# Gate row summed from two rounded parts, and square sums added by VectorE: a change to a hybrid linear-attention trunk on one Trainium2 core

## The chip, the cores and the metric

The kernel runs on one core of one Trainium2 chip. The metric is the device time of one execution in microseconds (us). Three runs of the kernel before gave 1219.83, 1215.38 and 1220.5 us; their median is 1219.83 us.

A core has five engines that work side by side, each through its own queue in order: TensorE (PE) for matrix products, with its weight loads listed as PEld; VectorE (DVE) and ScalarE (ACT) for elementwise work; GpSimd (POOL), which can also add and here mostly issues stores; SyncE (SP), which issues loads. They meet through semaphores. Where one engine's instruction waits, everything behind it in that engine's queue waits too.

## The reference, cut to what matters

```python
def reference(x, c, ada_w, ada_b, ...):
    c_act = silu(c)
    mod = c_act @ ada_w + ada_b
    shift, scale, gate = split(mod, 3)
    h = rms_norm(x, norm_w) * (1 + scale) + shift
    hq, hf, hi, hz, gq, gk, gv, gz, ga, mg = split(h @ w_in, IN_OFFSETS)
    y_h = hgrn2_branch(hq, hf, hi, hz, ...)   # 8 heads, one RMS norm over all 1024 columns
    y_g = gla_branch(gq, gk, gv, gz, ga, ...) # 4 heads of 256, an RMS norm in each head
    merged = sigmoid(mg[0]) * (y_h @ w_branch[0]) + sigmoid(mg[1]) * (y_g @ w_branch[1])
    x = x + gate * (merged @ w_out)
    return rms_norm(x, final_norm_w)
```

The sequence has 1024 rows of 1024 columns; everything is float32. Two pieces matter here. The row `gate` is the last third of `silu(c) @ ada_w + ada_b`, 1024 numbers. The two RMS norms of the branches need, for each row of the sequence, the sum of the squares of the heads' outputs.

## The kernel before

Large products are made from numbers split in two parts: `split` (lines 191 to 198) lets ScalarE round a tile to the type float32r (`hi`, line 196) and VectorE subtract that from the tile (`lo`, line 197). A product then takes three matmuls (hi·hi, hi·lo, lo·hi), each of them a single instruction in the trace. Tiles that are not split go to TensorE as plain float32.

The program has three stretches. First comes a prologue in a fixed order (up to about 110 us of the span), which makes the modulation and the first projections. Then `Stream.go` (line 884) runs a list of projection jobs on TensorE (lines 541, 600 to 602, 643 to 645). After each unit of a job, `weave` (line 895) lets side work go one step: the attention of the heads (`stream.side`), and behind it `stream.back`, which holds the gate row and the preparation of factors and weight sums. A generator's `yield n` asks for n units before its next step, so it sets where its next instructions come in the program. Last come the branch products (line 1343) and the output stage (line 1520). A scheduler then orders each engine's instructions; buffers are 46 slots of 4 KB per partition, taken in rotation by `Slots`.

Three places are touched.

- `gate_side` (lines 1044 to 1065) makes the gate row. SyncE loads eight tiles of `ada_w` (line 1050) and the bias row (line 1047). VectorE weights each tile by its part of `silu(c)` and sums the eight into `gacc` (lines 1052 and 1054). That leaves a sum over 128 partitions. TensorE does it in two halves of 512 columns by a matmul with a tile of ones (line 1062) and adds the bias by a matmul of one partition (line 1063), both in plain float32. ScalarE copies the result out (line 1064). `gate_b` is used much later, in `gate_wy` (line 1471).
- `gla_attention` (line 970): for each of four heads ScalarE squares the two halves of 128 columns (line 981), VectorE scales the outputs (line 982), and GpSimd adds the two tiles of squares (line 987). `inverse_root` (line 957) then splits the sum (lines 196 and 197), sums it over the partitions by two matmuls for each half with the float32r tile of ones, `ones_r` (lines 964 and 965), and takes the root.
- `hgrn_attention` (line 1086): for each of eight heads ScalarE squares (line 1095), VectorE scales (line 1096), and from the second head on GpSimd adds the squares to a running sum (line 1107). After the eighth, `inverse_root` follows.

Other VectorE work that is named below: lines 676 to 701 prepare a head's scores, line 953 multiplies a projection with its sigmoid, lines 1261, 1264 and 1286 are the second parts of the splits for the branch products, line 1166 makes factors.

Of the kernel before, what the change touches and what calls it, by code (L numbers as in the profile page):

```python
# [83 lines left out]
def hybrid_trunk_kernel(  # L84
# [6 lines left out]
    nc = tc.nc  # L91
# [9 lines left out]
    S = Slots(sp, N_SLOTS)  # L101
# [7 lines left out]
    def mtile():  # L109
        cnt[0] += 1  # L110
        return ps_m.tile([P, 512], F32, tag="m", name=f"pm{cnt[0]}")
# [6 lines left out]
    ones = cp.tile([P, P], F32, name="ones")  # L118
# [6 lines left out]
    ones_r = cp.tile([P, P], F32R, name="ones_r")  # L125
# [65 lines left out]
    def split(src, hi=None, lo=None):  # L191

        if hi is None:
            hi = S.get(list(src.shape[1:]), F32R)
            lo = S.get(list(src.shape[1:]), F32R)
        nc.scalar.copy(hi, src)  # L196
        nc.vector.tensor_sub(lo, src, hi.bitcast(F32))  # L197
        return hi, lo
# [715 lines left out]
    def put_act(acts, d, y):  # L914
        for half in range(2):
            nc.gpsimd.dma_start(acts[half][d // 2][:, d % 2 * 512:d % 2 * 512 + 512], y[:, half * 512:half * 512 + 512])
        S.free(y)
# [39 lines left out]
    def inverse_root(dst, sq, n):  # L957

        hi, lo = split(sq)
        yield 1  # L960
        for half in range(2):
            sl = slice(half * 512, half * 512 + 512)
            pn = mtile()
            nc.tensor.matmul(pn, ones_r, hi[:, sl], start=True, stop=False)
            nc.tensor.matmul(pn, ones_r, lo[:, sl], start=False, stop=True)
            nc.scalar.activation(dst[:, sl], pn, AF.Ln, bias=eps_t, scale=1.0 / n)
        nc.scalar.activation(dst, dst, AF.Exp, scale=-0.5)
        S.free(hi, lo)

    def gla_attention(h):  # L970
        qk = g_state
        v = qk.pop(("v", h))
        g = {}
        sq = {}

        def post(vh, half, po):
            if half == 0:
                g[vh] = qk.pop(("z", h, vh))
                sq[vh] = S.get([T])
            sl = slice(half * 512, half * 512 + 512)  # L980
            nc.scalar.activation(sq[vh][:, sl], po, AF.Square)
            nc.vector.scalar_tensor_tensor(g[vh][:, sl], po, vec[:, R_GN + vh:R_GN + vh + 1],
                                           g[vh][:, sl], ALU.mult, ALU.mult)

        yield from attention(qk.pop(("q", h)), qk.pop(("k", h)), alphas[h], lambda: v, 0, 256, post)
        S.free(*v)
        nc.gpsimd.tensor_add(sq[0], sq[0], sq[1])
        yield 1.5
        rst = sq[1]
        yield from inverse_root(rst, sq[0], 256)  # L990
        for half in range(4):
            sl = slice(half * 256, half * 256 + 256)
            for vh in range(2):
                nc.vector.tensor_mul(g[vh][:, sl], g[vh][:, sl], rst[:, sl])
            yield 1.5
        for vh in range(2):
            put_act(yg_d, 2 * h + vh, g[vh])
        S.free(*sq.values())
# [32 lines left out]
    for h in range(4):  # L1031
        if h >= 2:
            J.append(Feat(col(C_GK + h * P), rhs_h, gla_k_done(h)))
        J.append(Feat(col(C_GZ + h * 256), rhs_h, silu_done(g_state, ("z", h, 0))))
        J.append(Feat(col(C_GZ + h * 256 + P), rhs_h, silu_done(g_state, ("z", h, 1))))

        def v_done(v, h=h):
            g_state[("v", h)] = v
            start_side(gla_attention(h))
        J.append(Vblk(C_GV + h * 256, v_done))  # L1040
# [3 lines left out]
    def gate_side():  # L1044

        gacc, gbias = S.get([D]), S.get([D])
        nc.sync.dma_start(gbias[0:1, :], ada_b[0:1, 2 * D:3 * D])
        for k in range(KT):
            b = S.get([D])
            nc.sync.dma_start(b, ada_w[0, k * P:(k + 1) * P, 2 * D:3 * D])  # L1050
            if k == 0:
                nc.vector.tensor_scalar_mul(gacc, b, cs[:, 0:1])
            else:
                nc.vector.scalar_tensor_tensor(gacc, b, cs[:, k:k + 1], gacc, ALU.mult, ALU.add)
            S.free(b)
            yield 1
        yield 3
        gate_b[0] = S.get([D])
        for half in range(2):
            sl = slice(half * 512, half * 512 + 512)  # L1060
            pg = mtile()
            nc.tensor.matmul(pg, ones, gacc[:, sl], start=True, stop=False)
            nc.tensor.matmul(pg, ones[0:1, :], gbias[0:1, sl], start=False, stop=True)
            nc.scalar.copy(gate_b[0][:, sl], pg)
        S.free(gacc, gbias)


    h_state = {}
    ssq, rst_h = [None], [None]
# [16 lines left out]
    def hgrn_attention(h):  # L1086
        st = h_state
        y = [None]
        sq = [None]

        def post(vh, half, po):
            if half == 0:
                y[0], sq[0] = st.pop(("z", h)), S.get([T])
            sl = slice(half * 512, half * 512 + 512)
            nc.scalar.activation(sq[0][:, sl], po, AF.Square)
            nc.vector.scalar_tensor_tensor(y[0][:, sl], po, vec[:, R_HN + h:R_HN + h + 1],
                                           y[0][:, sl], ALU.mult, ALU.mult)

        yield from attention(st.pop(("q", h)), st.pop(("k", h)), st.pop(("f", h)), lambda: st[("v", h // 4)],
                             h % 4 * P, P, post, 4 if h % 4 == 1 else 3)  # L1100
        if h % 4 == 3:
            S.free(*st.pop(("v", h // 4)))
        put_act(yh_d, h, y[0])
        if ssq[0] is None:
            ssq[0] = sq[0]
        else:
            nc.gpsimd.tensor_add(ssq[0], ssq[0], sq[0])
            S.free(sq[0])
        if h == 7:
            yield 2  # L1110
            rst = S.get([T])
            yield from inverse_root(rst, ssq[0], D)
            S.free(ssq[0])
            rst_h[0] = rst

    def hgrn_v(h):
        def done(v):
            h_state[("v", h // 4)] = v
            if h == 0:
                stream.back.append([gate_side(), 4])  # L1120
        J.append(Vblk2(C_HI + h * P, done, lambda: start_side(hgrn_attention(h), 4)))

    for h in range(8):
        J.append(Feat(col(C_HQ + h * P), rhs_h, hq_done(h)))

        def f_done(ps, h=h):
            hf_done(h)(ps)
            if h % 4:
                start_side(hgrn_attention(h), 2)
        J.append(Feat(col(C_HF + h * P), rhs_h, f_done))  # L1130
        if h % 4 == 0:
            hgrn_v(h)
        J.append(Feat(col(C_HZ + h * P), rhs_h, silu_done(h_state, ("z", h))))
# [585 lines left out]
```

## Time and profile before

The profiled execution took 1216.46 us; its span, from the first instruction to the last, is 1214.8 us, so 1.7 us lie around it.

| | |
|---|---|
| median of three runs | 1219.83 us (1215.38 to 1220.5) |
| profiled execution, time and span | 1216.46 us, 1214.8 us |
| granted TensorE clock, mean | 0.998 |
| busy: TensorE, weight loads | 97 %, 81 % |
| busy: VectorE, ScalarE, GpSimd | 65 %, 45 %, 10 % |
| line 1062 and 1063, plain float32 | 2 matmuls each, 4 records each in the trace |

In the profile, a row of a timeline gives the start, the busy time, the engine, the line, the operation and the tiles, and in brackets how long the engine had been idle and what ended that. Busy times of one engine overlap, since the next instruction starts before the last result is written: what an instruction costs its engine is the step from its start to the next start. A row of waits reads: who waited for whom, the total, how many times, the longest.

### The profile page before, as it was taken

Reading aid. Unit: us, or ns where it says so; the run is one execution under the profiler, and the core shown is the slowest. Engines: PE = TensorE matmul, PEld = TensorE weight load, DVE = VectorE, ACT = ScalarE, POOL = GpSimd, SP = SyncE. Lnnn points to the kernel's source line nnn. Section 1 sums busy time; section 2 is a strip of 40 time slices with the busy share of each in tenths; the row PEclk is TensorE's granted clock in tenths of the full one; section 3 lists DMA queues with packets and bytes.
Section 4 is the critical chain, followed back from the end, with each engine's and each line's share of the span. In section 5 each row is a group of like instructions: output and inputs, shape, how many; then the busy total and the mean of one; then the engine's idle time right before and its main releaser. Section 6 shows DMA issues by size and latency. Waiting matters only on the chain.

```text
span 1214.8 us, 20860 instructions
## 1 busy us (share of the span) xinstructions
PE 1184.1 (97%) x8579; PEld 982.6 (81%) x8579; DVE 790.9 (65%) x1245; ACT 546.9 (45%) x797; POOL 123.8 (10%) x215
## 2 busy tenths in 40 slices
PE   5999999999999999999999999999999999999997
PEld 3777889889798888888887888877778888878886
DVE  4637444774848456877884365794653775988994
ACT  5646732434434244344332324455743544444554
POOL 4100000202111121121110101011220000000000
PEclk9999999999999999999999999999999999999999
DMA  9814000844444267255341112054697746435523
GB/s 320 277 70 139 18 19 19 293 141 161 156 152 149 66 207 249 94 179 169 108 174 47 59 53 70 36 174 158 227 343 277 260 160 208 135 104 173 174 104 122
DMA packets 130961, 183.51 MB, mean 151 GB/s; under 512 B 7467, under 2 KB 97633, under 8 KB 130866
## 3 DMA queue, kind: packets, MB, share of 16 engines
q1 hardware_dynamic: 117250, 136.87, 35.7%
q0 software_dynamic: 13568, 45.31, 9.6%
q8 instruction: 67, 1.10, 0.4%
q14 instruction: 28, 0.23, 0.1%
q10 hardware_dynamic: 48, 0.01, 0.0%
HBM read 132.87 MB, written 49.28 MB: 150 GB/s over the span
## 4 chain that ended last, share of the span: by engine, by line
PE 61%; issue 23%; DVE 3%; ACT 3%; POOL 2%; DMA 1%; POOLq 0%; ACTq 0%; DVEq 0%
PE pd L541 19%; PE pd L1343 9%; PE sc_ps L1343 5%; PE pm L1343 5%; PE pd L1520 3%; PE pd L643 2%; PE pd L644 2%; PE pd L645 2%; PE sc_ps L1520 2%; PE pm L848 1%; PE pd L352 1%; PE pm L829 1%; PE pm L850 1%; PE pm L1520 1%; PE sc_ps L352 1%
## 5 line engine op out<-in xcount | busy, mean ns | idle before, releaser
L541 PE MATMUL pd<-b,b 128*128 128x512 f32 x1632 | 387.4, 394 | 0.0
L541 PEld LDWEIGHTS pd<-b,b 128*128 128x128 f32 x1632 | 302.4, 188 | 64.8 <-issue 1.4
L1343 PE MATMUL pd<-b,b 128*128 128x512 f32 x720 | 173.7, 392 | 4.3 <-ACT b L1414 2.1
L1343 PEld LDWEIGHTS pd<-b,b 128*128 128x128 f32 x720 | 133.7, 188 | 35.7 <-ACT b L1414 3.2
L197 DVE TENSOR_TENSOR b<-b,b 128x1024 fp32r<-128x1024 f32 (+2 forms) x89 | 98.9, 1122 | 83.1 <-ACT b L196 65.4
L196 ACT CAST b<-b 128x1024 fp32r<-128x1024 f32 (+2 forms) x89 | 82.9, 948 | 92.1 <-DVE b L1199 14.6
L1286 DVE TENSOR_TENSOR b<-b,b 128x1024 fp32r<-128x1024 f32 x56 | 68.3, 1224 | 66.9 <-ACT b L1285 52.3
L1285 ACT CAST b<-b 128x1024 fp32r<-128x1024 f32 x56 | 58.3, 1050 | 73.9 <-PE pd L1343 20.6
L1343 PE MATMUL sc_ps<-b,b 128*128 128x512 f32 x324 | 79.4, 391 | 1.0 <-ACT scT L793 1.0
L600 PE MATMUL pd<-b,b 128*128 128x256 f32 x256 | 74.2, 290 | 0.0
L1264 DVE TENSOR_TENSOR b<-b,b 128x1024 fp32r<-128x1024 f32 x48 | 59.2, 1251 | 20.8 <-ACT b L1263 15.1
L602 PE MATMUL pd<-b,b 128*128 128x256 f32 x256 | 72.5, 283 | 0.0
L601 PE MATMUL pd<-b,b 128*128 128x256 f32 x256 | 72.4, 283 | 0.0
L1343 PEld LDWEIGHTS sc_ps<-b,b 128*128 128x128 f32 x324 | 60.3, 188 | 14.6 <-ACT scT L793 1.4
L1343 PE MATMUL pm<-b,b 128*128 128x512 f32 x300 | 72.1, 389 | 0.0
L1263 ACT CAST b<-b 128x1024 fp32r<-128x1024 f32 x48 | 49.9, 1050 | 41.2 <-PE pd L1343 16.0
L1343 PEld LDWEIGHTS pm<-b,b 128*128 128x128 f32 x300 | 56.3, 188 | 11.7
L352 PE MATMUL pd<-b,b 128*128 128x512 f32 x192 | 53.3, 410 | 2.0 <-ACT b L196 0.9
L1201 POOL DMA_DIRECT2D ws<-b x64 | 34.6, 541 | 192.0 <-DVE b L1195 86.5
L735 ACT COPY xb<-b 128x512 f32<-128x512 f32 x48 | 29.4, 620 | 49.4 <-PE sc_ps L715 26.7
L643 PE MATMUL pd<-b,b 128*128 128x512 f32 x128 | 51.3, 401 | 0.0
L644 PE MATMUL pd<-b,b 128*128 128x512 f32 x128 | 50.0, 390 | 0.0
(285 smaller groups left out, 1964.3 us busy)
## 6 DMA issues: line engine op xcount, KB each, us to landing
b<-in_w_in_dram SPq DMA_DIRECT2D x66, 512.0 KB, 4.2
ws<-b POOLq DMA_DIRECT2D x64, 256.0 KB, 3.3
b<-ws SPq DMA_DIRECT2D x32, 512.0 KB, 4.9
b<-in_x_dram SPq DMA_DIRECT2D x16, 512.0 KB, 5.7
b<-in_ada_w_dram SPq DMA_DIRECT2D x32, 256.0 KB, 6.9
b<-in_w_branch_dram SPq DMA_DIRECT2D x16, 512.0 KB, 4.4
b<-h SPq DMA_DIRECT2D x14, 512.0 KB, 4.3
wo<-b POOLq DMA_DIRECT2D x14, 512.0 KB, 5.7
```

The source lines that it names most:

```text
L196: nc.scalar.copy(hi, src)
L197: nc.vector.tensor_sub(lo, src, hi.bitcast(F32))
L352: nc.tensor.matmul(accs[f], wg(a, d, f), b[d][:, half * 512:half * 512 + 512], start=(d == 0 and n == 0), stop=(d == KT - 1 and n == 2))
L541: nc.tensor.matmul(ps[0:w, th * 512:(th + 1) * 512], a[:, k, 0:w], b[:, th * 512:(th + 1) * 512], start=(k == 0 and n == 0), stop=(k == KT ...
L600: nc.tensor.matmul(o, lh, hi[:, k % 4, :], start=(k == 0), stop=False)
L601: nc.tensor.matmul(o, lh, lo[:, k % 4, :], start=False, stop=False)
L602: nc.tensor.matmul(o, ll, hi[:, k % 4, :], start=False, stop=(k == KT - 1))
L643: nc.tensor.matmul(o, lh, hi[:, k % 2, :], start=(k == 0), stop=False)
L644: nc.tensor.matmul(o, lh, lo[:, k % 2, :], start=False, stop=False)
L1286: nc.vector.tensor_sub(lo, t, hi.bitcast(F32))
L1343: nc.tensor.matmul(o, a[:, sl], c, start=(p in (1, 5) and kt == 0 and n == 0), stop=(kt == 3 and n == 2), skip_group_check=True)
L1520: nc.tensor.matmul(o, a, b, start=(p in (1, 5) and kt == 0 and n == 0), stop=(kt == 3 and n == 2), skip_group_check=True)
```

## The change

The bias row is added to partition 0 of `gacc` by VectorE. `gacc` is then split, and each half of the column sums is two matmuls with `ones_r`, one for each part. The pause before them is 4 units where it was 3. The additions of squares at lines 987 and 1107 go from GpSimd to VectorE. Lines behind line 1057 stand three lines later in the changed kernel.

```diff
-        nc.gpsimd.tensor_add(sq[0], sq[0], sq[1])
+        nc.vector.tensor_add(sq[0], sq[0], sq[1])
...
-        yield 3
+        nc.vector.tensor_add(gacc[0:1, :], gacc[0:1, :], gbias[0:1, :])
+        hi, lo = split(gacc)
+        S.free(gacc, gbias)
+        yield 4
         gate_b[0] = S.get([D])
         for half in range(2):
             sl = slice(half * 512, half * 512 + 512)
             pg = mtile()
-            nc.tensor.matmul(pg, ones, gacc[:, sl], start=True, stop=False)
-            nc.tensor.matmul(pg, ones[0:1, :], gbias[0:1, sl], start=False, stop=True)
+            nc.tensor.matmul(pg, ones_r, hi[:, sl], start=True, stop=False)
+            nc.tensor.matmul(pg, ones_r, lo[:, sl], start=False, stop=True)
             nc.scalar.copy(gate_b[0][:, sl], pg)
-        S.free(gacc, gbias)
+        S.free(hi, lo)
...
-            nc.gpsimd.tensor_add(ssq[0], ssq[0], sq[0])
+            nc.vector.tensor_add(ssq[0], ssq[0], sq[0])
```

TensorE's queue at the gate row, before: the tiles `pm` are the two halves of the row, b_5918 is `gacc`, b_5919 the bias, and `pd` are the projections of a value block.

```order
L645 MATMUL pd_5955<-b_5711,b_158 128x512
L1062 MATMUL pm_6017<-b_5918,ones 128x512
L1063 MATMUL pm_6017<-b_5919,ones 128x512
L1062 MATMUL pm_6021<-b_5918,ones 128x512
L1063 MATMUL pm_6021<-b_5919,ones 128x512
L643 MATMUL pd_6026<-b_5699,b_143 128x512
```

The same place in the changed kernel, where b_5999 is `hi` and b_6000 `lo`:

```order
L645 MATMUL pd_5955<-b_5711,b_158 128x512
L643 MATMUL pd_6022<-b_5699,b_143 128x512
L644 MATMUL pd_6022<-b_5700,b_143 128x512
L645 MATMUL pd_6022<-b_5699,b_151 128x512
L643 MATMUL pd_6022<-b_5699,b_144 128x512
L644 MATMUL pd_6022<-b_5700,b_144 128x512
L645 MATMUL pd_6022<-b_5699,b_152 128x512
L1065 MATMUL pm_6030<-b_5999,ones_r 128x512
L1066 MATMUL pm_6030<-b_6000,ones_r 128x512
L1065 MATMUL pm_6034<-b_5999,ones_r 128x512
L1066 MATMUL pm_6034<-b_6000,ones_r 128x512
L643 MATMUL pd_6022<-b_5703,b_145 128x512
```

The four matmuls of the row have moved behind six matmuls of the next value block; the rest of TensorE's queue is in the same order as before.

VectorE's queue ahead of them, before, where the line 1054 rows sum the row into `gacc`:

```order
L1054 SCALAR_TENSOR_TENSOR b_5918<-b_5933,cs,b_5918 128x1024
L1096 SCALAR_TENSOR_TENSOR b_5489<-pm_5891,vec,b_5489 128x512
L686 TENSOR_TENSOR b_5669<-xb,b_5848 128x256x3
L688 TENSOR_TENSOR b_5848<-b_5848 128x256
L701 TENSOR_TENSOR tot_725<-b_5848 128x256
L1054 SCALAR_TENSOR_TENSOR b_5918<-b_5942,cs,b_5918 128x1024
L197 TENSOR_TENSOR b_6331<-b_5855,b_6330 128x1024
L1054 SCALAR_TENSOR_TENSOR b_5918<-b_5951,cs,b_5918 128x1024
```

And in the changed kernel, from the same instruction on to the split of `gacc` (line 1110 is the addition of squares that was at line 1107):

```order
L1054 SCALAR_TENSOR_TENSOR b_5918<-b_5933,cs,b_5918 128x1024
L1099 SCALAR_TENSOR_TENSOR b_5489<-pm_5891,vec,b_5489 128x512
L1110 TENSOR_TENSOR b_4458<-b_4458,b_5888 128x1024
L686 TENSOR_TENSOR b_5669<-xb,b_5848 128x256x3
L688 TENSOR_TENSOR b_5848<-b_5848 128x256
...
L1054 SCALAR_TENSOR_TENSOR b_5918<-b_5971,cs,b_5918 128x1024
L197 TENSOR_TENSOR b_6336<-b_5855,b_6335 128x1024
L1054 SCALAR_TENSOR_TENSOR b_5918<-b_5980,cs,b_5918 128x1024
L1054 SCALAR_TENSOR_TENSOR b_5918<-b_5989,cs,b_5918 128x1024
L1057 TENSOR_TENSOR b_5918<-b_5918,b_5919 1x1024
L197 TENSOR_TENSOR b_6000<-b_5918,b_5999 128x1024
```

Three instructions are new between the first term of the row and TensorE: an addition of squares (line 1110), the addition of the bias (line 1057) and the split's subtraction (line 197 into b_6000), which waits for a rounding on ScalarE. The split into b_6336 has moved behind the fifth of the seven line 1054 rows; before, it stood behind the second.

VectorE's queue at the start of the branch products, before and after the addition of the seventh head's squares; before:

```order
L1096 SCALAR_TENSOR_TENSOR b_7051<-pm_7354,vec,b_7051 128x512
L679 TENSOR_TENSOR xb<-xb,b_7329 128x32x8
L1286 TENSOR_TENSOR b_7443<-b_7181,b_7442 128x1024
L686 TENSOR_TENSOR b_7164<-xb,b_7329 128x256x3
L687 TENSOR_TENSOR b_7329<-b_7329 128x256
```

And in the changed kernel (line 1289 is the former line 1286):

```order
L1099 SCALAR_TENSOR_TENSOR b_7056<-pm_7359,vec,b_7056 128x512
L1110 TENSOR_TENSOR b_4458<-b_4458,b_7356 128x1024
L679 TENSOR_TENSOR xb<-xb,b_7334 128x32x8
L1289 TENSOR_TENSOR b_7448<-b_7186,b_7447 128x1024
L686 TENSOR_TENSOR b_7169<-xb,b_7334 128x256x3
```

The addition stands ahead of twelve instructions that end with line 953, and six of those twelve are splits for the branch products, as before.

## The prediction

> **What bounds the kernel now.** I read the page first: which engine is busy, and what the chain that ended last is made of.
>
> ```profile
> PE 1184.1 (97%) x8579; PEld 982.6 (81%) x8579; DVE 790.9 (65%) x1245; ACT 546.9 (45%) x797; POOL 123.8 (10%) x215
> PE 61%; issue 23%; DVE 3%; ACT 3%; POOL 2%; DMA 1%; POOLq 0%; ACTq 0%; DVEq 0%
> ```
>
> TensorE is busy for 97 % of the span, and 84 % of the last chain is TensorE or its issue. So what an instruction costs on TensorE's queue counts in full; what it costs elsewhere counts where TensorE waits for it. The waits of TensorE come second; these rows are the longest one and the two longest behind the prologue.
>
> ```profile
> PE pm L219 <- DVE b L210: 8.3, 4, 4.0
> ...
> PE pd L1343 <- ACT b L1414: 2.1, 2, 1.8
> PE pd L1343 <- DVE b L953: 1.5, 1, 1.5
> ```
>
> The first belongs to the prologue, which the change does not touch. The last is the only one of over 1 us for VectorE in the rest, and it matters below. Third is the timeline where the change is.
>
> **The gate row on TensorE.** Its queue at the row:
>
> ```profile
> 640.92 1.02 PE L1062 MATMUL pm<-b,ones 128*128 128x512 f32 x2
> 641.87 1.12 PE L1063 MATMUL pm<-b,ones 1*128 1x512 f32 x2
> 642.92 1.12 PE L1062 MATMUL pm<-b,ones 128*128 128x512 f32 x2
> 643.98 1.12 PE L1063 MATMUL pm<-b,ones 1*128 1x512 f32 x2
> 645.02 0.50 PE L643 MATMUL pd<-b,b 128*128 128x512 f32 x1
> 645.36 0.39 PE L644 MATMUL pd<-b,b 128*128 128x512 f32 x1
> ```
>
> Four plain float32 matmuls hold the queue from 640.92 to 645.02, 4.10 us, and the bias of one partition costs as much as the 128 (1.05 us). The next step is 0.34 us. The new form runs already in the eighth head's `inverse_root`:
>
> ```profile
> 854.39 0.40 PE L964 MATMUL pm<-b,ones_r 128*128 128x512 f32 x1
> 854.62 0.47 PE L965 MATMUL pm<-b,ones_r 128*128 128x512 f32 x1
> 854.93 0.40 PE L964 MATMUL pm<-b,ones_r 128*128 128x512 f32 x1
> 855.16 0.39 PE L965 MATMUL pm<-b,ones_r 128*128 128x512 f32 x1
> 855.39 4.28 PE L1343 MATMUL sc_ps<-b,b 128*128 128x512 f32 x18
> ```
>
> One step is 0.23 us, so the new four cost 0.92 us (1.00 with the small hold inside this group). The long step after the old row (0.34 against 0.23) goes as well. The term is 0.92 - 4.10 - 0.11 = **-3.3 us**.
>
> [...]
>
> **Does TensorE wait for the two parts?** The row now needs three more steps on VectorE and ScalarE. VectorE's rows before:
>
> ```profile
> 624.44 1.28 DVE L1054 SCALAR_TENSOR_TENSOR b<-b,cs,b 128x1024 f32<-128x1024 f32 x1
> 625.63 0.75 DVE L1096 SCALAR_TENSOR_TENSOR b<-pm,vec,b 128x512 f32<-128x512 f32 x1
> 626.29 2.51 DVE L686 TENSOR_TENSOR b<-xb,b 128x768 f32<-128x768 f32 x1
> ...
> 631.27 1.23 DVE L197 TENSOR_TENSOR b<-b,b 128x1024 fp32r<-128x1024 f32 x1
> 632.41 6.56 DVE L1054 SCALAR_TENSOR_TENSOR b<-b,cs,b 128x1024 f32<-128x1024 f32 x5
> ```
>
> `gacc` is done at 638.97. GpSimd's addition and the group of line 686 explain the long third row:
>
> ```profile
> 624.37 3.62 POOL L1107 TENSOR_TENSOR b<-b,b 128x1024 f32<-128x1024 f32 x1
> L686 DVE TENSOR_TENSOR b<-xb,b x12: 940/952/2508, 117.1 to 802.3; 128x768 f32<-128x768 f32 x12
> ```
>
> Line 686 takes 0.95 us in the median and 2.51 us here, next to an addition on GpSimd that ends at 627.99. So GpSimd's addition holds up VectorE's instruction, and with it gone line 686 gets back 1.56 us. In its place VectorE does the addition itself: one step of a tile of 1024, 631.27 to 632.41, is 1.14 us. The end of `gacc` moves to 638.97 + 1.14 - 1.56 = 638.55. [...]
>
> The trace has no addition over one partition; its bounds are 0 and the 1.22 us of a whole tile (below). I take 1.22, since TensorE's one-partition row cost as much as its full one. A rounding and its subtraction, and what ScalarE does at that time:
>
> ```profile
> 613.51 1.05 ACT L196 CAST b<-b 128x1024 fp32r<-128x1024 f32 x1
> 614.59 1.23 DVE L197 TENSOR_TENSOR b<-b,b 128x1024 fp32r<-128x1024 f32 x1 [5.55 <-ACT b L196]
> 641.12 1.01 ACT L648 COPY b<-pd 128x1024 f32<-128x1024 f32 x1 [9.86 <-PE pd L645]
> ```
>
> ScalarE was idle for 9.86 us up to 641.12, so it can round at once. Then `hi` is there at 638.55 + 1.22 + 1.05 = 640.8 and `lo` at 642.1. TensorE comes to the first new matmul six steps later than before, at 640.92 + 6 x 0.23 = 642.3, and needs `lo` at 642.5: no wait, with 0.4 us in hand. Ahead of the rounding on ScalarE stands one rounding that needs the third weighted tile, some 6 us earlier; behind it only the copy of line 648, whose bank is needed only a whole block of 48 matmuls later. If line 686 keeps its 2.51 us, `lo` comes at 643.6 and TensorE and all behind it wait 1.1 us: bounds 0 and +1.1, taken 0.
>
> **The eleven additions.** GpSimd before, and a same-sized addition on VectorE:
>
> ```profile
> L987 POOL TENSOR_TENSOR b<-b,b x4: 2390/2403/3028, 216.1 to 422.4; 128x1024 f32<-128x1024 f32 x4
> L1107 POOL TENSOR_TENSOR b<-b,b x7: 2395/2405/3617, 532.6 to 849.6; 128x1024 f32<-128x1024 f32 x7
> L1166 DVE TENSOR_TENSOR b<-b,b x8: 1214/1224/1227, 221.0 to 250.6; 128x1024 f32<-128x1024 f32 x8
> ```
>
> GpSimd loses at least 11 x 2.4 = 26 us of work, VectorE gains 11 x 1.14 = 12.5 us. The chain of squares gets 1.2 us shorter each time, but TensorE hardly waits at its end (no row of `inverse_root` is among its longer waits). In eleven stretches, each over one of GpSimd's additions, TensorE was busy all the time:
>
> ```profile
> sum 34.00, PE 34.00 PEld 29.37 DVE 26.15 ACT 12.90 POOL 30.90; mean PE 3.09 PEld 2.67 DVE 2.38 ACT 1.17 POOL 2.81
> ```
>
> So I count ten at nothing: VectorE has 65 % of the span busy, TensorE's queue covers it. If that cover is gone, each costs up to 1.14 us. No new addition waits long: each stands behind the scaling of the same output, which has waited for the same squares. GpSimd's stores no longer stand behind an addition, and SyncE's queue keeps its order but for one pair of loads near the first attention.
>
> The seventh head's addition is different. It stands ahead of the VectorE work for which TensorE waits:
>
> ```profile
> 798.04 2.75 POOL L1107 TENSOR_TENSOR b<-b,b 128x1024 f32<-128x1024 f32 x1
> 799.10 2.21 DVE L679 TENSOR_TENSOR xb<-xb,b 128x256 f32<-128x256 f32 x1
> 810.62 1.23 DVE L953 TENSOR_TENSOR b<-b,pd 128x1024 f32<-128x1024 f32 x1
> 811.90 3.47 PE L1343 MATMUL pd<-b,b 128*128 128x512 f32 x14 [1.49 <-DVE b L953]
> L679 DVE TENSOR_TENSOR xb<-xb,b x12: 637/656/2352, 115.9 to 799.1; 128x256 f32<-128x256 f32 x12
> 796.00:812.00 16.00, 14.51 (x125) 11.59 (x124) 15.97 (x18) 10.95 (x13) 3.79 (x3) 1.00 0.71 244
> ```
>
> In the last row the fourth number is VectorE: 15.97 of 16 us. Here VectorE is the bound, and TensorE stands for 1.49 us. The change adds 1.14 us there and gives back 2.21 - 0.66 = 1.55 us: **-0.4 us**; bounds +1.14 (nothing given back) and -1.5 (the wait gone).
>
> **Sum**: -3.3 - 0.4 = -3.7 us on the profiled execution: 1216.46 becomes 1212.8 us. The median of the three runs is 3.4 us above that execution, and the runs spread over 5.1 us; I carry the difference to the median: 1219.83 - 3.7 = **1216.1 us**, 0.3 % less.
>
> **The rivals.**
>
> - [...] Several of GpSimd's additions held VectorE; if without them TensorE's remaining waits in the body shrink too (1.49, 2.1 and smaller ones), up to 3 us more go: 1213 us. For: the long rows of 679 and 686. Against: ScalarE ends the 2.1.
> - *TensorE waits for the low part.* 1.1 us, and the 798 us place gives nothing: 1217.6 us. For: only 0.4 us in hand. Against: the row above.
> - *TensorE gains nothing by coming earlier.* The 3.3 us are given back at the next wait for a load, or the new form costs as much as the old: 1219.8 us. Against: lines 964 and 965, and waits that follow TensorE themselves.
> - *Slower: VectorE's queue becomes the bound.* The additions come ahead of what TensorE waits for, as they do at 798 us, and nothing is given back. All eleven would add 12.5 us, less 3.3: 1229 us. It decides from 0.3 us of TensorE wait for each addition, and passes 0.5 % at 0.86 us. For: the row from 796 to 812. Against: ten of the eleven places. [...]
>
> **How the numbers follow.** Forecast 50 %, more from the interface 18 %, the low part 15 %, nothing gained 12 %, slower 5 %. A measurement of this kernel tells about 0.5 % (6.1 us) from no change. Faster by more than that needs the first rival or a low median: 0.20; within 0.75; slower 0.05. The range reaches from the first rival with 2 us of run spread, 1211, to nothing gained with 1.2 us, 1221; the last rival is left out.
>
> **What would show it.** Right: lines 1065 and 1066 with one record each, four steps of about 0.23 us, no wait ahead of line 1066; lines 679 and 686 with no row over 1.2 us; TensorE's wait for line 953 at 1.1 us or less; 26 us or more less of GpSimd, and VectorE's busy time up by less than the 13 steps of 1.14 us (14.8 us) that it takes on, since long rows shrink. Wrong: a gap before line 1066, or new waits of TensorE for VectorE behind any of lines 987 and 1110.

## The result, and the profile after

The changed kernel takes **1212.3 us** (median of 12 runs, 1211.28 to 1215.76); the kernel before, on the same chip beside it, 1216.5 us (12 runs, 1214.52 to 1220.5). The ratio is 0.9967, with a 95 % interval of 0.9956 to 0.9979: 0.33 % or 4 us faster, where 3.7 us (0.30 %) was forecast. That is below the 0.5 % that I had named as the bound, so by my cases it is "within 0.5 %", but the interval leaves out 1.

The profiled execution of the changed kernel took 1213.82 us, with a span of 1212.1 us. Its busy times (engine, us, share of the span, instructions):

```profile
PE 1182.6 (98%) x8575; PEld 983.5 (81%) x8575; DVE 793.2 (65%) x1258; ACT 547.6 (45%) x798; POOL 95.5 (8%) x204
```

GpSimd (POOL) loses 28.3 us. VectorE took on thirteen steps of about 1.14 us, 14.8 us, and is busy only 2.3 us longer: 12.5 us came back from instructions that GpSimd's additions no longer hold up. Where they had been held, the groups of single lines (shortest/median/longest in ns) now show no long row:

```profile
L679 DVE TENSOR_TENSOR xb<-xb,b x12: 639/650/660, 115.8 to 795.8; 128x256 f32<-128x256 f32 x12
L686 DVE TENSOR_TENSOR b<-xb,b x12: 941/948/977, 117.0 to 797.5; 128x768 f32<-128x768 f32 x12
L1110 DVE TENSOR_TENSOR b<-b,b x7: 1203/1216/1225, 532.4 to 847.1; 128x1024 f32<-128x1024 f32 x7
```

The longest rows before were 2352 ns (679) and 2508 ns (686). The row on TensorE, from its timeline:

```profile
641.20 0.39 PE L1065 MATMUL pm<-b,ones_r 128*128 128x512 f32 x1
641.43 0.39 PE L1066 MATMUL pm<-b,ones_r 128*128 128x512 f32 x1
641.66 0.40 PE L1065 MATMUL pm<-b,ones_r 128*128 128x512 f32 x1
641.90 0.39 PE L1066 MATMUL pm<-b,ones_r 128*128 128x512 f32 x1
642.13 0.39 PE L643 MATMUL pd<-b,b 128*128 128x512 f32 x1
```

Four steps take 0.93 us, with no gap ahead of line 1066 and no long step behind. The steps that make the two parts, on VectorE and ScalarE:

```profile
637.40 1.21 DVE L1057 TENSOR_TENSOR b<-b,b 1x1024 f32<-1x1024 f32 x1
638.65 1.05 ACT L196 CAST b<-b 128x1024 fp32r<-128x1024 f32 x1 [6.48 <-DVE b L1057]
639.73 1.23 DVE L197 TENSOR_TENSOR b<-b,b 128x1024 fp32r<-128x1024 f32 x1 [1.11 <-ACT b L196]
```

The low part ends at 640.96 and is needed at 641.43: 0.47 us in hand. TensorE's waits, in the same columns as before:

```profile
PE pm L219 <- DVE b L210: 7.6, 4, 3.7
...
PE pd L1346 <- ACT b L1417: 2.4, 2, 2.1
...
PE pd L1346 <- DVE b L953: 1.0, 1, 1.0
```

The wait for line 953 fell from 1.5 to 1.0 us. The wait for ScalarE has grown a little, to 2.1 us at its longest; it is the longest behind the prologue. And here is something that no part of the change touches. Windows around it (TensorE, weight loads, VectorE, ScalarE, GpSimd, then granted clock, DMA share, GB/s):

```profile
888.00:890.50 2.50, 1.71 (x7) 1.44 (x8) 0.56 (x1) 0.60 (x1) 1.27 (x3) 0.97 1.05 410
890.50:893.50 3.00, 3.00 (x8) 2.35 (x8) 0.00 (x0) 0.88 (x1) 0.00 (x0) 0.50 1.02 397
893.50:896.50 3.00, 3.00 (x14) 2.44 (x14) 1.23 (x1) 1.27 (x3) 0.54 (x1) 0.96 0.99 323
```

Behind that wait the granted clock is 0.50 for 3.4 us (890.3 to 893.7): eight matmuls step by 0.43 us instead of 0.23, which loses 1.6 us. Before's profile kept 1.00 behind the same wait, which was 1.8 us long there. So this execution shows 2.7 us less span than before's; with those 1.6 us added, I estimate 4.3 without the fall.

Where the time went is read by putting the starts of the same TensorE instructions of both traces side by side (changed kernel less before, us):

| stretch of the span | change | what stands there |
|---|---|---|
| up to 120 us | -0.1 | prologue, not touched |
| 312 to 314 | -0.7 | wait of line 715 for line 718, gone |
| 549 to 552 | -0.3 | a smaller step in an attention |
| the row, 641 | **-3.3** | four plain matmuls for four of float32r |
| 809 to 813 | -0.5 | wait for line 953 |
| 836 to 862 | +0.5 | longer steps, one of them a 0.2 us wait for ScalarE |
| 886 to 900 | +1.9 | wait for ScalarE +0.3, clock fall +1.6 |

Every other stretch differs by 0.2 us or less.

### The profile page after: what moved, and what is told of

The parts are those of the page before. It is cut to its first block, busy times and chain, and to the rows that moved or that the text cites. A ratio compares the mean times of both kernels' runs of the same rounds, so it can differ in the third digit from the quotient of the medians.

```text
span 1212.1 us, 20836 instructions
## 1 busy us (share of the span) xinstructions
PE 1182.6 (98%) x8575; PEld 983.5 (81%) x8575; DVE 793.2 (65%) x1258; ACT 547.6 (45%) x798; POOL 95.5 (8%) x204
## 4 chain that ended last, share of the span: by engine, by line
issue 54%; PE 35%; POOL 4%; DMA 3%; DVE 2%; ACT 1%; SPq 0%; POOLq 0%; ACTq 0%; DVEq 0%
PE pd L1346 9%; PE sc_ps L1346 5%; PE pm L1346 5%; PE pd L541 3%; PE pd L1523 3%; POOL ws L1204 2%; PE sc_ps L1523 2%; PE pm L1523 1%; PE pd L602 1%; PE pd L601 1%; PE pd L600 1%; PE pd L352 1%; DMA b<-in_ada_w_dram 1%; POOL yh L916 1%; DMA yg<-b 1%
## 5 line engine op out<-in xcount | busy, mean ns | idle before, releaser
L1289 DVE TENSOR_TENSOR b<-b,b 128x1024 fp32r<-128x1024 f32 x56 | 68.1, 1221 | 69.7 <-ACT b L1288 49.6
L1346 PEld LDWEIGHTS pm<-b,b 128*128 128x128 f32 x300 | 56.8, 189 | 11.9
```

What stands on the lines that cost most here:

```text
L1289: nc.vector.tensor_sub(lo, t, hi.bitcast(F32))
L1346: nc.tensor.matmul(o, a[:, sl], c, start=(p in (1, 5) and kt == 0 and n == 0), stop=(kt == 3 and n == 2), skip_group_check=True)
```

## The experiments

Before was timed beside each group of kernels; its medians were 1216.34 us (18 runs) for the first four, 1217.14 us (24 runs) for the next four and 1216.45 us (18 runs) for the last three.

**The row alone.**

```diff
-        nc.vector.tensor_add(sq[0], sq[0], sq[1])
+        nc.gpsimd.tensor_add(sq[0], sq[0], sq[1])
...
-            nc.vector.tensor_add(ssq[0], ssq[0], sq[0])
+            nc.gpsimd.tensor_add(ssq[0], ssq[0], sq[0])
```

> Only the gate row is changed (bias added by VectorE, two rounded parts); the eleven additions of squares stay on GpSimd. Theory (each step on TensorE's queue counts in full): the row's term alone, -3.3 us, ratio about 0.9973. GpSimd's addition still holds line 686 at about 2.5 us, but VectorE has no addition of its own there: the low part comes at about 642.5 us and TensorE waits at most 0.1 us for it. TensorE's waits at line 715 (0.7 us) and for line 953 (1.5 us) stay as before. Rival (the gain is given back at the next wait): no gain, ratio 1.000.

1212.53 us (8 runs), ratio 0.9973 (0.9963 to 0.9983). So the row carries the gain. Its profile holds a small surprise: TensorE, GpSimd and VectorE near the row.

```profile
623.63 2.44 POOL L1110 TENSOR_TENSOR b<-b,b 128x1024 f32<-128x1024 f32 x1
623.74 3.42 DVE L1054 SCALAR_TENSOR_TENSOR b<-b,cs,b 128x1024 f32<-128x1024 f32 x1
641.55 0.40 PE L1065 MATMUL pm<-b,ones_r 128*128 128x512 f32 x1
642.37 0.50 PE L1066 MATMUL pm<-b,ones_r 128*128 128x512 f32 x1 [0.43 <-DVE b L197]
```

Here TensorE does wait for the low part: 0.82 us from one matmul to the next, 0.59 too many, where I had expected 0.1 at most. GpSimd's addition started 0.11 us ahead of line 1054 and VectorE's instruction took 3.42 us instead of 1.28. In before's profile the two started within 0.07 us (GpSimd 624.37, VectorE 624.44), and there line 1054 took its 1.28 us, GpSimd's addition 3.62 instead of 2.4, and line 686 behind them 2.51 instead of 0.95. So in one profile VectorE's instruction is the long one of the pair, in the other GpSimd's. The waits at line 715 (0.6 us) and for line 953 (1.4 us) stay, as expected.

**The additions alone.** The edit is the two `tensor_add` lines of the change in the kernel before.

> Only the eleven additions of squares go to VectorE; the gate row stays plain float32 in one pass of four matmuls. Theory of the prediction: -0.4 us, all of it in TensorE's wait for line 953. Theory after the changed kernel's trace: -1.4 us, 0.7 at line 715 in the second head, 0.3 before 552 us, 0.4 at line 953. Rival (VectorE's queue is the bound): slower, up to +12.5 us.

1216.72 us (11 runs), ratio 1.0001 (0.9992 to 1.001): nothing gained to be told from noise; the -0.4 us of the first theory lies inside the interval (-1.0 to +1.2 us), the -1.4 of the second does not. By the starts of TensorE's instructions its profile gains 0.7 us at 313 and 0.3 at 550, and loses 0.7 at 809 to 813 and 0.7 at 833 to 862. The last loss is not the additions': the profile of the row alone, in which GpSimd still adds, loses 1.2 us there. VectorE is busy no longer than before (790.9 us), though it has eleven instructions more:

```profile
PE 1184.7 (97%) x8579; PEld 982.5 (81%) x8579; DVE 790.8 (65%) x1256; ACT 546.9 (45%) x797; POOL 95.6 (8%) x204
```

Side by side with before, eight of its old instructions, each next to one of GpSimd's additions there, take 1.0 to 1.7 us less, 11.9 us in all; the eleven new steps are 12.5 us. So VectorE's queue did not get longer. At the place where I had forecast a gain:

```profile
811.81 1.16 PE L1343 MATMUL pd<-b,b 128*128 128x512 f32 x4 [1.62 <-DVE b L953]
813.26 4.85 PE L1343 MATMUL pd<-b,b 128*128 128x512 f32 x20 [0.29 <-ACT b L1317]
```

Line 953's result comes as late as before (the wait is 1.62 us, was 1.49), and a second wait, for ScalarE, follows that before's profile did not have. In the whole change the same wait was 1.04. Both kernels have the same order on VectorE here, but in this one a rounding on ScalarE waits 2.17 us for a load (0.64 us in the changed kernel), and VectorE stands idle for its result ahead of line 953:

```profile
805.20 1.05 ACT L1263 CAST b<-b 128x1024 fp32r<-128x1024 f32 x1 [2.17 <-DMA b<-fx]
808.18 1.23 DVE L1264 TENSOR_TENSOR b<-b,b 128x1024 fp32r<-128x1024 f32 x1 [0.54 <-ACT b L1263]
```

Without these 0.54 us the wait would, as an estimate, have been 1.08 (1.62 - 0.54). So what this place gives depends on when that load arrives.

**Each addition done in two dependent instructions**, the second leaving the value as it is.

```diff
-        nc.vector.tensor_add(sq[0], sq[0], sq[1])
+        nc.vector.tensor_add(sq[1], sq[0], sq[1])
+        nc.vector.tensor_max(sq[0], sq[0], sq[1])
...
-            nc.vector.tensor_add(ssq[0], ssq[0], sq[0])
+            nc.vector.tensor_add(sq[0], ssq[0], sq[0])
+            nc.vector.tensor_max(ssq[0], ssq[0], sq[0])
```

> The changed kernel with each of the eleven additions on VectorE done in two instructions of the same size (the sum into the other tile, then the maximum of the running sum and that sum, which is the same number because squares are not negative). Theory (TensorE's queue covers VectorE but for the seventh head and the chain of squares at line 715): 1 to 2.5 us slower than the changed kernel, TensorE's wait for line 953 longer by about 1.1 us. Rival (VectorE is the bound at all eleven places): 12.5 us slower than the changed kernel, which makes it 8 us slower than the kernel before.

1225.21 us (5 runs), ratio 1.0077 (1.0065 to 1.009): nearly 13 us over the changed kernel, the rival's price. But TensorE's waits name another cause than a full VectorE:

```profile
PE pm L964 <- ACT b L196: 5.9, 2, 4.8
...
PE pm L965 <- DVE b L197: 2.5, 3, 1.2
```

These are the matmuls of `inverse_root`, which no longer hide behind TensorE's queue. The timeline shows the longest, at the eighth head (an addition's later end puts line 196 behind line 1290 in ScalarE's queue, and that one waits for a load):

```profile
862.22 1.04 ACT L1290 CAST b<-b 128x1024 fp32r<-128x1024 f32 x1 [5.55 <-DMA b<-ws]
863.17 1.04 ACT L196 CAST b<-b 128x1024 fp32r<-128x1024 f32 x1
864.26 0.80 PE L964 MATMUL pm<-b,ones_r 128*128 128x512 f32 x2 [4.81 <-ACT b L196]
864.86 1.91 PE L1348 MATMUL sc_ps<-b,b 128*128 128x512 f32 x4
```

The last row has 0.43 us for each matmul: behind this wait of 4.81 us the clock is down again, 0.60 in the mean from 864 to 868 us.

**The same time on VectorE, without a later result**: a second addition behind each, into a tile that nobody reads any more.

```diff
         nc.vector.tensor_add(sq[0], sq[0], sq[1])
+        nc.vector.tensor_add(sq[1], sq[1], sq[1])
...
             nc.vector.tensor_add(ssq[0], ssq[0], sq[0])
+            nc.vector.tensor_add(sq[0], sq[0], sq[0])
```

> The changed kernel, with a further addition of the same size on VectorE right behind each of the eleven, into a tile that nobody reads any more (its values are left out of nothing that is computed). VectorE's queue gets the same 11 x 1.14 = 12.5 us as when each addition was done in two dependent steps, but no result comes later by itself. Theory that the earlier 12.8 us came from the later end of the chain of squares (ScalarE's rounding and the two matmuls behind it): the queue's time alone is hidden at ten places, and at the seventh head's TensorE's wait for line 953 grows by up to 1.1 us, so 0 to 1.5 us over the changed kernel, 1212.3 to 1214, ratio to before 0.997 to 0.998. Rival, VectorE's queue is the bound: again about 12 us, 1224 to 1225, ratio 1.007.

1217.22 us (12 runs), ratio 1.0002 (0.9991 to 1.0012): about 4 us over the changed kernel. Neither theory: a third of the 12.5 us shows. TensorE's rows say at which places:

```profile
313.12 0.89 PE L715 MATMUL sc_ps<-xb,b 128*32 128x48 f32 x64 [1.76 <-DVE tot L718]
...
568.54 1.83 PE L829 MATMUL pm<-b,b 128*128 128x128 f32 x14 [0.56 <-ACT b L808]
597.45 0.89 PE L715 MATMUL sc_ps<-xb,b 128*32 128x48 f32 x64 [0.40 <-DVE tot L718]
854.43 0.50 PE L965 MATMUL pm<-b,ones_r 128*128 128x512 f32 x1 [1.03 <-DVE b L197]
```

With the step between the row's first two matmuls (0.3 too long here) these are 4.1 us. At the seventh head the wait for line 953 is 1.04 us, as in the changed kernel, so the growth that I had expected did not come. If 4 us are what VectorE's time costs, the rest of the 13 us is the later end of the chain of squares. The profile of the kernel with two dependent instructions agrees: by the starts of TensorE's instructions it loses some 12 us against the changed kernel at the four places of `inverse_root` (two of them with the clock down there: 0.50 from 363 to 366 us, 0.60 from 864 to 868), and 3.6 elsewhere. Half of the 12 comes from the one place where a rounding stands behind a late load.

**The plain row, made twice on end** (each pass begins with a matmul that has `start=True`, and the run's output was the row once, not doubled as the expectation says).

```diff
-            nc.tensor.matmul(pg, ones, gacc[:, sl], start=True, stop=False)
-            nc.tensor.matmul(pg, ones[0:1, :], gbias[0:1, sl], start=False, stop=True)
+            for _ in range(2):
+                nc.tensor.matmul(pg, ones, gacc[:, sl], start=True, stop=False)
+                nc.tensor.matmul(pg, ones[0:1, :], gbias[0:1, sl], start=False, stop=True)
```

> The kernel before with the gate row's four plain float32 matmuls issued twice into the same bank, so that the row is summed twice (the output row is double). Theory (what stands in TensorE's queue counts in full): +4.1 us, ratio about 1.0034. Rival (later waits swallow a shift of that size): less than +2 us.

1223.24 us (4 runs, 1221.05 to 1228.62), ratio 1.0063 (1.0042 to 1.0085): 7.7 us more, not 4.1. TensorE's timeline in the profiled run, which is the longest of the four, from the fourth matmul on:

```profile
643.39 1.12 PE L1064 MATMUL pm<-b,ones 1*128 1x512 f32 x2
644.44 1.76 PE L1063 MATMUL pm<-b,ones 128*128 128x512 f32 x2
646.13 2.07 PE L1064 MATMUL pm<-b,ones 1*128 1x512 f32 x2
648.13 2.07 PE L1063 MATMUL pm<-b,ones 128*128 128x512 f32 x2
650.13 2.07 PE L1064 MATMUL pm<-b,ones 1*128 1x512 f32 x2
652.13 0.80 PE L643 MATMUL pd<-b,b 128*128 128x512 f32 x1
```

The first four take 4.11 us (640.33 to 644.44), the second four 7.69. From 644 to 656 us the granted clock is 0.57 in the mean, though TensorE is busy all the time. That 7.69 is also the mean excess of the four runs is chance: this run is 12.1 us over before's profile, 9.0 of them at the row and 2.5 at the seventh head, and the mean granted clock of its span is 0.992 (0.998 in before).

**The plain row, made twice and apart.**

```diff
+        for rep in range(2):
-        for half in range(2):
+          for half in range(2):
...
+          yield 12
```

> The kernel before, with the plain float32 row made twice, the second time about 16 us (72 float32r matmuls) behind the first. Theory that the second four matmuls in a row cost 7.7 us instead of 4.1 because the granted clock fell after the first four: apart, each four run at the full clock, so 4.1 to 4.3 us over before, 1220.5, ratio 1.0035, and the granted clock stays at 1.00 in both stretches. Rival, a doubled row costs more for another reason (its tile, its copy, the buffers held longer): again 7.7 us, 1224, ratio 1.0063.

1221.94 us (5 runs), ratio 1.0034 (1.0022 to 1.0046): 4.1 us more (2.7 to 5.6), as the theory has it, and not the rival's 7.7. One detail is against the expectation: the clock did not stay up behind the first row. Windows of this kernel:

```profile
640.00:644.00 4.00, 4.00 (x9) 1.01 (x8) 0.00 (x0) 1.58 (x3) 0.00 (x0) 1.00 0.00 0
644.00:648.00 4.00, 4.00 (x11) 3.15 (x12) 0.00 (x0) 0.57 (x1) 0.00 (x0) 0.57 0.00 0
...
664.00:668.00 4.00, 4.00 (x10) 1.45 (x9) 3.40 (x13) 2.44 (x4) 0.00 (x0) 1.00 0.00 0
668.00:672.00 4.00, 4.00 (x17) 2.85 (x16) 1.23 (x1) 1.18 (x2) 0.00 (x0) 1.00 0.49 131
```

The clock fell behind the first row (0.57 from 644 to 648 us) and not behind the second (1.00 from 664 to 672). Behind the first, eight matmuls of the next block step by 0.43 us, about 1.6 us lost; the profile of before, and that with the additions alone, show no such fall (1.00 from 640 to 649 us in both). Against before, this profile is 1.6 us longer at the first row and 4.3 at the second; it is 1.8 us shorter elsewhere, most of that ahead of the rows, so that its whole excess of 4.1 us matches one row partly by chance.

**The pause of before.**

```diff
-        yield 4
+        yield 3
```

> The changed kernel with the pause of 3 units that the kernel before had: the row's four matmuls stand six matmuls earlier in TensorE's queue. Theory, that TensorE waits for the low part by the margin that is left: in the changed kernel's profile the low part was there 0.47 us before it was needed, in two other executions of the same instructions 0.2 to 0.5 us too late; six steps of 0.23 us earlier TensorE waits 0.9 us at the first matmul of line 1066 (up to 1.9 us where a load is late), and none at line 1065 for the high part. Rival, the splits are so early that the pause does nothing: no gap, four steps of 0.23 us.

One run, 1215.75 us, which tells nothing by itself; the timeline does.

```profile
640.44 0.50 PE L1065 MATMUL pm<-b,ones_r 128*128 128x512 f32 x1 [0.41 <-ACT b L196]
641.70 0.50 PE L1066 MATMUL pm<-b,ones_r 128*128 128x512 f32 x1 [0.76 <-DVE b L197]
```

TensorE waits for the high part too, which I had not expected: two loads of the row's weights were late by 0.39 and 0.26 us in VectorE's rows. The steps that end at these two matmuls, 0.79 and 1.26 us, are 1.6 us over two of 0.23. So I estimate the fourth unit of pause at about 0.9 us where the loads are in time (six steps of 0.23 less the 0.47 in hand), and at more where they are late.

**The changed kernel again**, no edit.

> The changed kernel itself, to stand beside the kernels of this call on the same chip. Theory: as measured first, ratio to before 0.9967 (0.9956 to 0.9979), 1212 to 1213. Its profile tells whether the low part comes in time again: the step between lines 1065 and 1066 is 0.23 us if so, and up to 0.7 us if a load of the row's weights is late.

1212.57 us (10 runs), ratio 0.9971 (0.9962 to 0.9981). The low part came a little late this time:

```profile
640.90 0.40 PE L1065 MATMUL pm<-b,ones_r 128*128 128x512 f32 x1
641.38 0.50 PE L1066 MATMUL pm<-b,ones_r 128*128 128x512 f32 x1
```

0.48 us from one to the next, 0.25 too many, and here as well loads of the row were late (0.42 and 0.26 us). The mean granted clock is 0.998, where the first profile has 0.997, and the span is 1210.7 us.

**Three tries at a better kernel.** The second loads of w_out later; loads further ahead; and the first with a longer pause ahead of the row. Each starts from the changed kernel.

```diff
-(((0, 3, 0), (0, 6), (0, 7)), ((1, 1, 2), (1, 5), (1, 6)))
+(((0, 3, 0), (0, 6), (0, 7)), ((1, 2, 1), (1, 5), (1, 6)))
```

> The changed kernel, with the second set of four loads of w_out (1 MB) issued two pairs later. TensorE's longest wait behind the prologue, 2.1 us near 887 us, is for a rounding on ScalarE that waits for a load of w_in, in a stretch where the DMA engines are busy all the time. Theory that these loads of w_out take that load's place in the queues: with them later the wait falls below 1 us and the fall of the granted clock behind it (1.6 us) goes too, 1 to 3 us less, 1209 to 1211, ratio to before 0.994 to 0.996. Rival, the stores fill that stretch anyway, or the later loads are then waited for: 1212 to 1214, ratio 0.997 to 0.998.

```diff
-                    ahead(2 * n + i // 2, 4, 2)
+                    ahead(2 * n + i // 2, 5, 2)
```

> The changed kernel, with the loads of the branch products' tiles issued up to five pairs ahead instead of four. Theory that the same wait near 887 us comes from a load that is issued too late: issued one pair earlier (about 3.4 us), it lands before the rounding needs it, and 1 to 3 us go, 1209 to 1211, ratio to before 0.994 to 0.996. Rival, the DMA engines are full there, so an earlier issue only makes another load late, or the held buffers delay the preparation: 1212 to 1216, ratio 0.997 to 1.000.

```diff
-        yield 4
+        yield 6
...
-(((0, 3, 0), (0, 6), (0, 7)), ((1, 1, 2), (1, 5), (1, 6)))
+(((0, 3, 0), (0, 6), (0, 7)), ((1, 2, 1), (1, 5), (1, 6)))
```

> The changed kernel with a pause of 6 units ahead of the row and the second loads of w_out two pairs later. Theory: the wait for the low part (0 to 0.5 us by execution) goes for good, and the wait near 887 us with its fall of the granted clock gets smaller, together 1 to 2 us less than the changed kernel: 1210 to 1211.5, ratio to before 0.995. Rival: neither is to be told from the changed kernel, ratio 0.996 to 0.998.

Later loads: 1212.51 us (5 runs), ratio 0.9957 (0.9945 to 0.9969). With the longer pause as well: 1212.93 us (8 runs), ratio 0.9972 (0.9962 to 0.9982). Neither is to be told from the changed kernel: the first ratio lies in its theory's range, but its interval takes in 0.9967, and the same edit with the longer pause gives the rival's ratio. The wait near 887 us is 1.5 us and 1.6 instead of 2.1, not below 1. Behind it, with the later loads alone, the next twelve matmuls step by 0.24 us, so no clock fall follows there; the mean granted clock is 0.998 in both profiles, as in the changed kernel's second one with a wait of 1.8. Loads further ahead: 1216.86 us (12 runs), ratio 0.9994 (0.9984 to 1.0005), the rival's result. Its timeline shows the wait moved, not gone (at 887 there is none now):

```profile
887.12 3.03 PE L1346 MATMUL pd<-b,b 128*128 128x512 f32 x12
...
902.86 2.58 PE L1346 MATMUL pd<-b,b 128*128 128x512 f32 x10 [2.28 <-DVE b L1289]
```

With the longer pause the row's four steps are 0.23 us each again, as they should be; the few tenths that this can give are below what the runs tell apart.

## Why the prediction was right, point by point

**The row, -3.3 us: right in mechanism and size.** The old four took 4.10 us and a long step of 0.11 beyond a usual one; the new four take 0.93 (641.20 to 642.13), which is -3.28. The row alone measures 0.9973, or 3.3 us of 1216.3, and a second plain row, put apart, costs 4.3 us in its profile: one row's time, once more. One thing was not in the sum: the clock fell to 0.50 behind one of the two plain rows that stood apart, and it did not fall in the profiles of before and of the additions alone (1.00 up to 649 us). Where it falls, the new row saves, as an estimate from the eight steps of 0.43 us there, some 1.6 us more. How often it falls without a profile is open.

**The wait for the low part: the right neighbourhood, too sure.** The forecast margin was 0.4 us, and the first profile shows 0.47. Both sides of it came 1.1 us earlier than forecast (the low part at 640.96 instead of 642.1), since VectorE and TensorE alike reach this stretch 1.1 us earlier than before. The addition over one partition took 1.21 us, as taken. But other executions of the same instructions show no margin: 0.25 us lost in the second profile of the changed kernel, 0.2 with loads further ahead and 0.5 with the later loads of w_out. The step that fell short is the reading of when the row's sum is done from one execution: loads of its weights, 0.65 to 0.8 us late in these three profiles, were put at no scatter. The 0.6 us of the row alone has another cause, GpSimd's addition that held line 1054 for 2.1 us. The bounds of 0 and 1.1 us held them all.

**Line 686 and 679: right.** No row is over 0.98 us, and 12.5 of VectorE's 14.8 us came back, with the eight instructions that the additions alone show as held. The kernel with the row alone adds that either engine's instruction can be the long one: VectorE's line 1054 took 3.42 us there beside an addition of 2.44, and in before 1.28 beside one of 3.62. What decides which, their starts within about 0.1 us do not tell, and no run tests it.

**Ten additions at nothing: the sum right, the reason too simple.** The additions alone measure 1.0001. But "TensorE's queue covers it" was drawn from eleven windows in which TensorE was busy. The kernel with idle additions shows that a third of such VectorE time reaches TensorE, at five places where it waits for VectorE's next result, once by way of ScalarE. In the change itself nothing had to be covered: over the eleven places VectorE got back about what it took on, because GpSimd's additions had held it at eight of them and not only at the two that I counted. In the profile, the wait of line 715 near 313 us is gone; the rows of before and after:

```profile
313.46 0.89 PE L715 MATMUL sc_ps<-xb,b 128*32 128x48 f32 x64 [0.66 <-DVE tot L718]
```

```profile
312.81 0.89 PE L715 MATMUL sc_ps<-xb,b 128*32 128x48 f32 x64
```

This gain comes by way of a load. VectorE's queue ahead of that wait holds up for a load of w_in in before:

```profile
301.72 0.69 DVE L1195 TENSOR_TENSOR b<-b 128x512 f32<-128x512 f32 x1 [0.71 <-DMA b<-in_w_in_dram]
```

The row alone has the same stop (0.74 us) and keeps the wait; both kernels with the additions on VectorE have neither. Why the load is no longer waited for was not tested.

**The seventh head, -0.4 us: right in the changed kernel's profiles, not shown by the times.** The wait for line 953 went from 1.49 to 1.04 us in the changed kernel, -0.45. In the kernel with the additions alone it stayed (1.62). The price by itself was right: without VectorE's stop of 0.54 us for a late rounding it would have been 1.08 there too. That it comes out at TensorE depends on a load, and 0.4 us is less than the runs tell apart.

**The rivals.** The first, more time from what GpSimd's additions had held, did not come about, though its time, 1213 us, is nearer to the measured one than mine. Both were counted from 1219.83 us, and the row alone, with GpSimd still adding, takes 1212.53. The line with the chances speaks of an "interface", which no run shows; the additions alone show eight VectorE instructions 1.0 to 1.7 us shorter, 11.9 us in all, and the eleven additions, 12.5 us, used that up. "TensorE gains nothing by coming earlier" is ruled out by the row alone, whose interval ends at 0.9983. "TensorE waits for the low part" came about in part, with 0.2 to 0.5 us instead of 1.1. "Slower: VectorE's queue becomes the bound" was priced at 12.5 us for eleven additions. The additions alone cost nothing, since their time came back. Time that does not come back costs: doubled additions nearly 13 us, but mostly by latency and clock, and idle ones a third of it, 4 us or 0.36 for each. That is about the threshold of 0.3 us, and the kernel with idle additions comes out at before's time.

**The total.** -3.7 us was forecast and about -4 measured, which the interval of 2.6 to 5.4 us (0.9979 and 0.9956 of 1216.5) does not tell apart. The predicted time itself is 3.8 us above the measured one, mostly because I carried the sum to a median of three runs that lay 3.3 us above that of all twelve (1216.5; later sets have 1216.3 to 1217.1 us). That the time fell into the range of 1211 to 1221 us says little, since no change would have done so too; the kernels with one part of the change each say more. The near match of the whole is partly luck: the profile has -3.3 and -0.5 us as forecast, but also -1.0 at two places and losses of 0.5 and 1.9 that were in no sum.

## What to carry to other kernels

On the engine that sets the time, count an instruction by its step in the queue and by its type: here one plain float32 matmul of 128x512 cost 4.5 steps of a float32r one (1.03 us against 0.23), and one partition as much as 128 (1.05 us each). A margin of a few tenths of a microsecond that is read from one execution is none (0.47 us in hand in one profile here, 0.25 lost in the next); look for the loads ahead of it, or give the order one unit more. And an engine that is busy 65 % of the time is not free: here eleven additions cost nothing because VectorE got their time back, and as much again without that return cost 4 us.

## What the runs showed of the hardware that was not expected

- **The clock fell with TensorE busy.** Behind 4.1 us of plain float32 matmuls the granted clock went to 0.50 in two of five cases: behind the first of the rows apart (0.50 from 644.8 to 646.8 us) and in the row made twice (0.50 from 648 to 652). Behind the second of the rows apart, in before and with the additions alone it was 1.00. In the row made twice it was, by the steps, down from 644.8 to 655.0 us, and the last three plain matmuls took 2.0 us each instead of 1.05.
- **It stayed down for 3.4 us, or three times that.** Behind the first of the rows apart, the steps are 0.43 us from 644.2 to 647.6, 3.4 us; behind the 2.1 us wait near 887 us it was down for 3.4 us (890.3 to 893.7), and in the row made twice for 10.2, three times as long. What sets the length, these three falls do not show, and what decides between the two rows apart stays open.
- **A wait of 2.1 us cost 3.7.** The wait near 887 us was 2.08 us long in the changed kernel's first profile, and the clock fell to 0.50 behind it, which lost 1.6 us more. With the pause of before it was 2.1 too, and the mean granted clock of that span is 0.996. It was 1.82 in before, and the clock stayed at 1.00 (893 to 899 us). Length alone does not decide: behind the wait of 2.28 us near 903 us, with loads further ahead, the next ten matmuls step by 0.24 us and the twelve behind them by 0.23, so no fall follows there.
